# The first LayerNorm of an encoder layer: scale and offset with tokens as rows on half the columns, and the first loads in one queue

## The chip, the cores and the metric

The kernel runs on one core of a Trainium2 chip. The metric is the device time of one execution in microseconds (us). Times before and after come from repeated executions; a profile comes from one execution recorded by the hardware profiler.

## The reference

The input x holds 512 tokens of 1024 numbers. The reference computes:

```
x = layer_norm(x, ln_in_g, ln_in_b)                  # this case
h = x @ w_in                                         # q, k, v, latents, gates
a = differential attention, 4 heads                  # part A
b = latent attention, 8 heads, own low-rank q, kv    # part B
c = dilated window attention, 3 groups of 4 heads    # part C
y = sum over branches of sigmoid(g + b_gate) * (branch @ w_branch)
x = layer_norm(alpha * x + y @ w_out)
x = layer_norm(alpha * x + moe(x))                   # 16 experts, top 2, and a shared one

layer_norm(x, g, b) = (x - mean) * rsqrt(var + 1e-5) * g + b
```

Only the first line is computed differently. Its output is used twice: as input of the projections, and in the residual sum alpha * x.

## The kernel before

The tokens lie in 4 chunks of 128 (`NT`), the 1024 columns in 8 blocks of 128 (`KB`). For a projection TensorE needs the normed x with columns as partitions, in a high and a low part of float32r: `xh` and `xl`, 128 x 8 x 512 each. A product is three matmuls (`mm3`, lines 133 to 135): high by high, high by low weights, low by high weights. Weights come from DRAM and are split in the same way: ScalarE copies the high part, VectorE or GpSimd subtracts for the low part.

The start (`ln_in`, `start_step`) runs an order written out by hand, the string `START`. A step has a letter, a chunk c and, for some, a half g of the columns (g = 0 is columns 0 to 511, named `och`; g = 1 is `ocl`):

- X loads a chunk (two DMAs on SP's queue), s takes statistics, r and q work out mean and 1/sqrt (r ends with a square root on ScalarE, q goes on with it on VectorE).
- n (ScalarE) computes (x - mean) / std in place. t transposes four blocks on TensorE into a PSUM bank. u (ScalarE) or U (VectorE) applies scale and offset, which are one number for each partition by then, to one block of 128 x 128 at a time, from PSUM into SBUF. h copies into `xh`, l or L subtracts into `xl`.
- W loads a third of the weight `w_b1` (1008, 1008 and 672 columns), w and v or V split it. m multiplies a chunk with it: 8 blocks of 3 matmuls of 336 columns, 24 for a chunk. e copies the result out.
- K steps run helpers: constants, loads of small vectors, masks, tables of the rotary embedding. Z stores the chunk, without scale and offset, in DRAM (`xn_dram`) for the residual.

After `START` follow `steps`, which walks `PLAN` (parts A, B, C; `P0` is the first block of values, `v_block(0)`, two banks of 48 matmuls of 256 columns), and `FILL`, work that has no hurry: the gates (G and g, 24 matmuls of 512 columns each into the one bank `gm`), branch projections (O, B) and the residual steps (R). From `START` on, a scheduler places these instructions by its own estimates; each engine then runs its list strictly in order. R0 to R7 (`residual`) read a chunk and half of `xn_dram`, multiply by the scale and add the offset on GpSimd, and store it again.

SP, ScalarE and GpSimd each have a queue that issues DMAs in order.

## Time and profile before

| | us |
|---|---|
| times of 3 runs | 942.04, 946.68, 946.85 |
| median | 946.68 |
| the profiled execution's own time | 947.56 |
| its span | 945.8 |
| TensorE busy | 888.0 (94%) |
| VectorE, ScalarE, GpSimd busy | 639.0, 458.1, 230.5 |
| mean granted TensorE clock | 0.985 of full speed |

The span is what the profiler sees from the first to the last instruction. The time of the execution is 1.8 us longer. TensorE is idle for 57.8 us of the span, and the lists of views that follow tell where.

### The profile page before, as it was taken

The page shows a single profiled execution, that of the slowest core. Times are in us where ns is not written, and L with a number is a line of the kernel's source. Part 1 is how long each engine was busy: PE and PEld are TensorE (multiplying, and loading weights), DVE is VectorE, ACT ScalarE, POOL GpSimd, SP SyncE. Part 2 cuts the span into 40 slices and gives each one's busy share as a digit, 9 for nine tenths or more (in the row PEclk, how much of TensorE's full clock was granted, in tenths as well). Part 3 has the DMA queues.
Part 4 walks back from the last instruction along what each step waited for, and adds up shares of the span by engine and source line. Part 5 has one row for each costly group of instructions (what it writes and reads, how often), then busy time and mean ns, then how long its engine had stood idle before and what let it go on. Part 6 is the DMA issues. An engine that isn't in the chain of part 4 may idle for free.

```text
span 945.8 us, 13734 instructions
## 1 busy us (share of the span) xinstructions
PE 888.0 (94%) x4916; PEld 737.6 (78%) x4916; DVE 639.0 (68%) x1316; ACT 458.1 (48%) x797; POOL 230.5 (24%) x220
## 2 busy tenths in 40 slices
PE   4899999978998999999999999899999899999994
PEld 3889988767877988877989889788998666667762
DVE  6757885535678777955756586737775667676776
ACT  6645755445366544642433254333334555566632
POOL 2122140031020013003323336504033212111033
PEclk9999999989999999998999999999999999999998
DMA  7343443243348444444664558468556599999962
GB/s 263 117 137 109 146 125 106 90 125 106 119 150 246 127 154 134 150 129 115 170 190 128 147 183 262 161 217 308 191 198 247 190 336 359 361 403 388 389 205 90
DMA packets 61287, 183.74 MB, mean 194 GB/s; under 512 B 9088, under 2 KB 9520, under 8 KB 53920
## 3 DMA queue, kind: packets, MB, share of 16 engines
q1 hardware_dynamic: 50912, 147.84, 47.5%
q0 software_dynamic: 9584, 32.88, 9.3%
q10 hardware_dynamic: 720, 2.11, 0.6%
q8 instruction: 40, 0.66, 0.3%
q14 instruction: 31, 0.25, 0.1%
HBM read 139.18 MB, written 31.82 MB: 181 GB/s over the span
## 4 chain that ended last, share of the span: by engine, by line
PE 52%; DVE 7%; issue 7%; DMA 6%; ACT 2%; POOL 2%; SPq 0%; ACTq 0%; POOLq 0%; DVEq 0%
PE mm L1495 11%; PE sc L1521 7%; PE mm L133 5%; PE mm L134 5%; PE mm L135 5%; PE gm L133 2%; PE gm L134 2%; PE gm L135 2%; DMA w<-ys_dram,r 1%; PE tr L599 1%; PE tr L363 1%; PE sc L134 1%; PE sc L133 1%; PE sc L135 1%; DMA g_dram<-gt 1%
## 5 line engine op out<-in xcount | busy, mean ns | idle before, releaser
L171 DVE TENSOR_TENSOR w<-w,w 128x1024 fp32r<-128x1024 f32 (+5 forms) x97 | 155.6, 1621 | 51.0 <-ACT w L170 50.8
L170 ACT ACTIVATE w<-w 128x1024 fp32r<-128x1024 f32 (+5 forms) x99 | 122.2, 1263 | 58.1 <-PE mm L134 21.4
L134 PE MATMUL mm<-w,xh 128*128 128x256 f32 (+1 forms) x384 | 111.4, 290 | 0.2 <-DVE w L433 0.2
L133 PE MATMUL mm<-w,xh 128*128 128x256 f32 (+1 forms) x384 | 111.5, 291 | 0.0
L135 PE MATMUL mm<-w,xl 128*128 128x256 f32 (+1 forms) x384 | 111.2, 290 | 0.1
L1495 PE MATMUL mm<-w,xgh 128*128 128x512 f32 x320 | 100.9, 397 | 0.0
L134 PEld LDWEIGHTS mm<-w,xh 128*128 128x128 f32 x384 | 73.8, 192 | 1.4 <-DVE w L433 0.5
L133 PEld LDWEIGHTS mm<-w,xh 128*128 128x128 f32 x384 | 73.7, 192 | 1.1 <-ACT w L429 0.3
L135 PEld LDWEIGHTS mm<-w,xl 128*128 128x128 f32 x384 | 73.7, 192 | 0.9 <-DVE xl L472 0.5
L1521 PE MATMUL sc<-w,hT 128*128 128x512 f32 x160 | 73.2, 599 | 0.0
L1495 PEld LDWEIGHTS mm<-w,xgh 128*128 128x128 f32 x320 | 58.4, 188 | 11.0
L133 PE MATMUL mm<-xh,w 128*128 128x512 f32 x160 | 63.7, 398 | 0.9 <-DVE V L171 0.9
L134 PE MATMUL mm<-xl,w 128*128 128x512 f32 x160 | 63.6, 397 | 0.0
L135 PE MATMUL mm<-xh,w 128*128 128x512 f32 x160 | 63.3, 396 | 0.0
L1495 PE MATMUL mm<-w,xgl 128*128 128x512 f32 x160 | 62.5, 390 | 0.0
L170 ACT ACTIVATE pth<-tr 128x512 fp32r<-128x512 f32 x80 | 41.6, 548 | 35.4 <-PE tr L599 35.3
L588 ACT ACTIVATE e<-sc,nm 128x512 f32<-128x512 f32 x64 | 43.6, 685 | 29.9 <-DVE nm L659 17.0
L171 DVE TENSOR_TENSOR ptl<-tr,pth 128x512 fp32r<-128x512 f32 x80 | 48.8, 629 | 12.8 <-ACT pth L170 12.4
L170 ACT ACTIVATE T<-T 128x512 fp32r<-128x512 f32 (+1 forms) x36 | 22.7, 629 | 61.3 <-POOL T L571 39.0
L950 POOL DMA_DIRECT2D g_dram<-gt x24 | 13.7, 571 | 156.7 <-ACT gt L941 115.6
L1521 PEld LDWEIGHTS sc<-w,hT 128*128 128x128 f32 x160 | 29.0, 190 | 29.3 <-issue 27.7
L170 ACT ACTIVATE ghi<-graw 128x512 fp32r<-128x512 f32 x40 | 23.6, 625 | 52.3 <-PE gm L134 33.6
(445 smaller groups left out, 2284.6 us busy)
## 6 DMA issues: line engine op xcount, KB each, us to landing
w<-in_w_exp SPq DMA_DIRECT2D x48, 1024.0 KB, 7.7
graw<-in_w_gate SPq DMA_DIRECT2D x48, 256.0 KB, 3.0
T<-T SPq DMA_DIRECT2D x90, 128.0 KB, 2.5
w<-in_w_qk SPq DMA_DIRECT2D x20, 512.0 KB, 3.9
g_dram<-gt POOLq DMA_DIRECT2D x40, 256.0 KB, 3.2
w<-in_w_v SPq DMA_DIRECT2D x16, 512.0 KB, 4.0
ys_dram<-ys POOLq DMA_DIRECT2D x13, 512.0 KB, 7.8
gt<-g_dram SPq DMA_DIRECT2D x24, 256.0 KB, 2.8
```

The costliest lines, as they stand in the source:

```text
L133: nc.tensor.matmul(out, lh, rh, start=start, stop=False)
L134: nc.tensor.matmul(out, lh, rl, start=False, stop=False)
L135: nc.tensor.matmul(out, ll, rh, start=False, stop=stop)
L170: nc.scalar.activation(hi, src, AF.Copy)
L171: (eng or nc.vector).tensor_sub(lo, src, hi.bitcast(F32))
L363: nc.tensor.transpose(o.bitcast(FR), s.bitcast(FR), self.idr)
L588: nc.scalar.activation(out, src, AF.Exp, bias=nmax, scale=scale, accum_out=sm)
L599: nc.tensor.transpose(p[:, kb * 128:(kb + 1) * 128], e[:, kb * 128:(kb + 1) * 128], self.idf)
L950: self.nc.gpsimd.dma_start(self.g_dram[n // 8, n % 8, 0], self.gate(n, t == "g"))
L1495: self.nc.tensor.matmul(p, x[:, kb], y, start=kb == 0 and i == 0, stop=kb == KB - 1 and i == 2)
L1521: self.nc.tensor.matmul(y, hT[:, k], w[:, k, cs], start=k == 0, stop=k == 1)
```

## The change

For half g = 0 the scale and offset are applied while tokens are still rows. There they differ from column to column, so each must stand in all 128 partitions. A new step R loads the first 512 numbers of both vectors as one row (two KB each) by ScalarE's queue; b multiplies a column of ones by that row on TensorE, which leaves the row in all partitions of a PSUM bank (scale in `pv`, offset in `gm`). Then y computes (x - mean) * scale and z computes that * (1/std) + offset, both on VectorE with 128 x 512 elements. Steps n and u fall away for this half: the transposed block is final, so h and l read it from PSUM. Half g = 1 goes the old way, with u on ScalarE for all four chunks.

What Z stores for half 0 is then final, and R0 to R3 leave `FILL`. The loads of x and of `w_b1` are the first 12 DMAs of SP's queue; the small vectors and `lam` are issued by GpSimd. The chunks' matmuls (m) are cut at block 3 instead of 4, take the two `mm` banks in turn for all four chunks, and stand between the steps of the next chunk. The low parts of the weights come from GpSimd for all three thirds.

```
--- before.py
+++ after.py
@@ -47,7 +47,7 @@
 THETA = 500000.0
 DT = ()
 WIDE = (21,23)
-START = ("K0 G0 X0 s0 r0 q0 W0 w0 n01 X1 t01 X2 s1 W1 n00 r1 q1 u01 K1 n11 s2 t00 u00 n10 t10 X3 W2 V0 r2 q2 w1 V1 h00 s3 n20 l00 h01 u10 l01 r3 h10 t11 n21 t20 w2 v2 m00 U11 h11 L10 m01 q3 t21 m10 U20 U21 n31 n30 t31 L11 t30 h20 h21 l20 u31 U30 h30 h31 L21 m11 l30 m20 m21 l31 m30 m31 e0 e1 e2 e3 Z00 Z01 Z10 Z11 Z20 Z21 Z30 Z31")
+START = ("R0 X0 X1 G0 W0 K0 X2 W1 X3 W2 K6 K1 a0 b0 b1 s0 r0 y0 q0 z0 n01 s1 w0 t00 V0 h00 r1 t01 s2 u01 w1 q1 V1 y1 h01 l00 w2 z1 m00 n11 l01 V2 r2 t10 y2 t11 h10 q2 m01 u11 l10 z2 h11 m10 s3 n21 e0 t20 l11 t21 h20 r3 m11 y3 u21 l20 q3 z3 h21 m20 e1 n31 l21 t30 t31 h30 m21 u31 l30 h31 m30 e2 l31 m31 e3 K9 Z00 Z01 Z10 Z11 Z20 Z21 Z30 Z31")
 
 
 def ROPE(nc):
@@ -55,9 +55,9 @@
 
 
 RES = 4
-PLAN = ("k6 k2 P0 k3 k5 k7 L0 K0 K1 A0 K2 K3 L1 A1 P1 K4 K5 A2 k8 K6 K7 N T A3 J0 Q0 Y0 Q1 J1 Q2 H0 H1 Q3 Y1 k4 H2 H3 P2 H4 H5 K8 K9 H6 H7 P3 K12 K13 C0 K10 K11 P4 C1 K14 K15 P5 K18 K19 P6 C2 F K16 K17 P7 C3")
-
-FILL = ("G2 G0 g1 g3 G4 g5 G6 g7 G8 g13 g11 O0 G10 g9 O1 G12 O2 g15 O3 B2 B1 G14 B3 B0 g17 O4 G16 O5 O6 O7 B5 B7 B4 B6 / R0 R1 R2 R3 R4 R5 R6 R7 G18 g19 g21 g23 G22 G20")
+PLAN = ("P0 k2 k3 k5 k7 L0 K0 K1 A0 K2 K3 L1 A1 P1 K4 K5 A2 k8 K6 K7 N T A3 J0 Q0 Y0 Q1 J1 Q2 H0 H1 Q3 Y1 k4 H2 H3 P2 H4 H5 K8 K9 H6 H7 P3 K12 K13 C0 K10 K11 P4 C1 K14 K15 P5 K18 K19 P6 C2 F K16 K17 P7 C3")
+
+FILL = ("G2 G0 g1 g3 G4 g5 G6 g7 G8 g13 g11 O0 G10 g9 O1 G12 O2 g15 O3 B2 B1 G14 B3 B0 g17 O4 G16 O5 O6 O7 B5 B7 B4 B6 / R4 R5 R6 R7 G18 g19 g21 g23 G22 G20")
 LAST = ("r0 r1 Q00 Q01 Q02 Q03 c l3 l4 l5 m0 s0 u0 m1 s1 u1 w3 m2 x0 y0 l6 i0 s2 u2 b3 m3 x1 y1 l7 i1 s3 u3 b4 m4 x2 y2 s4 u4 b5 m5 x3 y3 s5 u5 b6 m6 x4 y4 s6 U6 b7 m7 x5 y5 i2 s7 U7 x6 y6 i3 x7 y7 A00 A01 A02 r2 e r3 g Q10 Q11 Q12 Q13 B00 B01 B02 P03 Q20 Q21 Q22 Q23 P10 P11 P12 P13 Q30 Q31 Q32 Q33")
 ORDER = ("u0 m u1 P20 P21 P30 a0 A0 P22 g0 P31 a1 A1 P23 g1 P32 T0 a2 A2 P33 b g2 a3 T1 A3 R0 M0 g3 R1 c T2 s0 N0 R2 f0 s1 T3 M1 R3 r N1 M2 f1 h0 N2 k o0 M3 i0 f2 h1 o1 N3 i1 S10 f3 D0 X h2 S11 h3")
 E0 = 4
@@ -209,12 +209,12 @@
 
     def cols(self, name, n, src=None):
         t = self.cp.tile([128, n], F32, name="v_" + name)
-        self.nc.sync.dma_start(t, self.a[name] if src is None else src)
+        self.nc.gpsimd.dma_start(t, self.a[name] if src is None else src)
         return t
 
     def loads(self):
         self.pos = self.cp.tile([128, NT], I32, name="pos")
-        self.nc.sync.dma_start(self.pos, self.a["positions"])
+        self.nc.gpsimd.dma_start(self.pos, self.a["positions"])
         self.inv = self.cols("inv_freq", 24, self.a["inv_freq"].to_broadcast([128, 24]))
 
     def loads2(self):
@@ -222,8 +222,11 @@
         self.dng = self.cols("diff_norm_g", 1)
         self.qng = self.cols("mla_q_norm_g", 3)
         self.kng = self.cols("mla_kv_norm_g", 2)
-        self.lam = self.T().bitcast(F32)[:, :256].rearrange("p (a b) -> p a b", a=4)
-        self.nc.sync.dma_start(self.lam, self.a["lam"].to_broadcast([128, 256]))
+
+    def scales(self):
+        nc = self.nc
+        nc.vector.tensor_scalar(self.hbg, self.hbg, 0.5, None, op0=OP.mult)
+        nc.vector.tensor_scalar(self.dng, self.dng, 1.0 - LAM_INIT, None, op0=OP.mult)
 
     def rope_tables(self):
 
@@ -334,9 +337,9 @@
         self.mk = mk
 
     def vectors(self):
-        nc, cp, lam = self.nc, self.cp, self.lam
-        nc.vector.tensor_scalar(self.hbg, self.hbg, 0.5, None, op0=OP.mult)
-        nc.vector.tensor_scalar(self.dng, self.dng, 1.0 - LAM_INIT, None, op0=OP.mult)
+        nc, cp = self.nc, self.cp
+        lam = self.T().bitcast(F32)[:, :256].rearrange("p (a b) -> p a b", a=4)
+        nc.gpsimd.dma_start(lam, self.a["lam"].to_broadcast([128, 256]))
         pr = self.T().bitcast(F32)[:, :128].rearrange("p (a b) -> p a b", a=2)
         nc.vector.tensor_mul(pr, lam[:, 0:4:2, :], lam[:, 1:4:2, :])
         sm = cp.tile([128, 2], F32, name="lam_s")
@@ -408,11 +411,36 @@
             return lp.tile([128, n], F32, name=f"{name}{c}")
 
         if t == "K":
-            (self.consts, self.loads, self.vectors, self.rope_tables, self.masks, self.rope_sin, self.loads2, self.rope_T, self.rope_L)[c]()
+            (self.consts, self.loads, self.vectors, self.rope_tables, self.masks, self.rope_sin, self.loads2, self.rope_T, self.rope_L, self.scales)[c]()
         elif t == "X":
             d["x", c] = [self.op.tile([128, S], FR, name=n, bufs=4).bitcast(F32) for n in ("och", "ocl")]
             for i in range(2):
-                nc.sync.dma_start(d["x", c][i], a["x"].rearrange("(i c) d -> c i d", c=NT)[c][:, i * 512:(i + 1) * 512])
+                nc.sync.dma_start(
+                    d["x", c][i], a["x"].rearrange("(i c) d -> c i d", c=NT)[c][:, i * 512:(i + 1) * 512])
+        elif t == "R":
+
+            d["gb"] = lp.tile([128, 2, 512], F32, name="gb")
+            nc.scalar.dma_start(d["gb"][0:1], a["ln_in"].rearrange("p (a b) -> p a b", a=2)[:, :, :512])
+            d["one"] = lp.tile([128, 128], F32, name="one")
+            v.memset(d["one"], 1.0)
+        elif t == "a":
+
+            nc.scalar.activation(small("sq"), d["one"][:, 0:1], AF.Sqrt)
+        elif t == "b":
+
+            d["b", c] = (self.pv_bank, self.gm_bank)[c]()
+            nc.tensor.matmul(d["b", c], d["one"][0:1], d["gb"][0:1, c], start=True, stop=True)
+        elif t == "y":
+            x = d["x", c][0]
+            v.scalar_tensor_tensor(x, x, d["mv", c][:, 0:1], d["b", 0], op0=OP.subtract, op1=OP.mult)
+        elif t == "z":
+            x = d["x", c][0]
+            v.scalar_tensor_tensor(x, x, d["rs", c], d["b", 1], op0=OP.mult, op1=OP.add)
+        elif t == "p":
+
+            d["warm"] = d.get("warm") or self.sc_bank()
+            for _ in range(c):
+                nc.tensor.matmul(d["warm"][:, :128], self.idf, self.idf, start=True, stop=True)
         elif t == "G":
             d["gc"] = lp.tile([128, 2, KB], F32, name="gc")
             nc.scalar.dma_start(d["gc"], a["ln_in_c"].rearrange("p (a b) -> p a b", a=2))
@@ -423,7 +451,8 @@
             else:
                 d["W", c] = [self.wstart(a["w_b1"][:, c * 1008:(c + 1) * 1008], 1008)[:, :1008]]
         elif t == "w":
-            d["w", c] = [self.slot_tile(i)[:, :1008 if c < 2 else 672] for i in (1, 2)]
+            d["w", c] = [(self.slot_tile(i + 1) if c < 2 else self.wp.tile([128, 1024], FR, name=n, bufs=1))[:, :1008 if c < 2 else 672]
+                         for i, n in enumerate(("ghi", "glo"))]
             for i, w in enumerate(d["W", c]):
                 n = w.shape[1]
                 nc.scalar.activation(d["w", c][0][:, i * n:(i + 1) * n], w, AF.Copy)
@@ -473,8 +502,8 @@
         elif t == "Z":
             nc.sync.dma_start(self.xn_dram[c][:, g * 512:(g + 1) * 512], d["x", c][g])
         elif t == "m":
-            p = d["m", c] = d.get(("m", c)) or (self.mm_bank, self.mm_bank, self.pv_bank, self.gm_bank)[c]()
-            for kb in range(4 * g, 4 * g + 4):
+            p = d["m", c] = d.get(("m", c)) or self.mm_bank()
+            for kb in range(3) if g == 0 else range(3, KB):
                 w = d["w", kb // 3]
                 self.mm3(p[:, :336], self.xh[:, kb, sl], self.xl[:, kb, sl], w[0][:, kb % 3], w[1][:, kb % 3], kb == 0, kb == KB - 1)
         elif t == "e":

```

Which instructions stand where is told by each engine's list.

SP's queue, from its first DMA, before (`och`, `ocl` are halves of a chunk, `w0` a third of `w_b1`):

```order
L415 DMA och_91<-in_x 128x512
L415 DMA ocl_92<-in_x 128x512
L212 DMA v_b_gate_433<-in_b_gate 128x24
L212 DMA v_diff_norm_g_435<-in_diff_norm_g 128x1
L212 DMA v_mla_q_norm_g_437<-in_mla_q_norm_g 128x3
L212 DMA v_mla_kv_norm_g_439<-in_mla_kv_norm_g 128x2
L153 DMA w0_111<-in_w_b1 128x1008
L415 DMA och_117<-in_x 128x512
L415 DMA ocl_118<-in_x 128x512
L415 DMA och_126<-in_x 128x512
L415 DMA ocl_127<-in_x 128x512
L153 DMA w0_134<-in_w_b1 128x1008
```

SP's queue after:

```order
L418 DMA och_87<-in_x 128x512
L418 DMA ocl_88<-in_x 128x512
L418 DMA och_91<-in_x 128x512
L418 DMA ocl_92<-in_x 128x512
L153 DMA w0_97<-in_w_b1 128x1008
L418 DMA och_105<-in_x 128x512
L418 DMA ocl_106<-in_x 128x512
L153 DMA w0_109<-in_w_b1 128x1008
L418 DMA och_111<-in_x 128x512
L418 DMA ocl_112<-in_x 128x512
```

The six small loads between the loads of x and `w_b1` are gone from this queue, and the second chunk stands ahead of the first weights.

VectorE, from the statistics of the third chunk, before (`st` statistics, `mv` mean and variance, `rs_y` 1/std, `nm` -mean/std):

```order
L438 BN_STATS st_159<-ocl 128x6
L234 CAST posf<-pos 128x4
L440 BN_AGGR mv_160<-st_159 128x2
L106 TENSOR_SCALAR rs_v<-mv_160 128x1
L113 RECIPROCAL rs_y<-rs_y 128x1
L116 TENSOR_SCALAR rs_t<-rs_y 128x1
L118 TENSOR_SCALAR rs_t<-rs_t,rs_v 128x1
L120 TENSOR_SCALAR rs_y<-rs_t,rs_y 128x1
L450 TENSOR_SCALAR nm_198<-mv_160,rs_y 128x1
L438 BN_STATS st_205<-och 128x6
L438 BN_STATS st_205<-ocl 128x6
L472 TENSOR_TENSOR xl<-u,xh 128x4x128 x2
```

VectorE after, from the statistics of the third chunk:

```order
L467 BN_STATS st_181<-och 128x6
L467 BN_STATS st_181<-ocl 128x6
L113 RECIPROCAL rs_y<-rs_y 128x1
L116 TENSOR_SCALAR rs_t<-rs_y 128x1
L237 CAST posf<-pos 128x4
L118 TENSOR_SCALAR rs_t<-rs_t,rs_v 128x1
L120 TENSOR_SCALAR rs_y<-rs_t,rs_y 128x1
L479 TENSOR_SCALAR nm_197<-mv_157,rs_y 128x1
L435 SCALAR_TENSOR_TENSOR och<-och,mv_157,pv 128x512
L501 TENSOR_TENSOR xl<-tr,xh 128x4x128
L438 SCALAR_TENSOR_TENSOR och<-och,rs_y,gm 128x512
L501 TENSOR_TENSOR xl<-u,xh 128x4x128
```

The first `xl` stood behind the statistics of all four chunks. Now it stands behind those of three, and behind the second chunk's first scaling step.

TensorE, its first rows, before (`tr`, `sc` banks for transposes, `mm` the product):

```order
L457 MATMUL tr<-idf,ocl 128x128 x4
L457 MATMUL tr<-idf,och 128x128 x4
L457 MATMUL sc<-idf,och 128x128 x4
L457 MATMUL sc<-idf,ocl 128x128 x4
L457 MATMUL tr<-idf,och 128x128 x4
L133 MATMUL mm<-w_113,xh 128x336
L134 MATMUL mm<-w_114,xh 128x336
L135 MATMUL mm<-w_113,xl 128x336
```

TensorE after (`gb` the row of scale and offset, `one` the ones):

```order
L432 MATMUL pv<-gb,one 128x512
L432 MATMUL gm<-gb,one 128x512
L486 MATMUL tr<-idf,och 128x128 x4
L486 MATMUL tr<-idf,ocl 128x128 x4
L133 MATMUL mm<-w_160,xh 128x336
L134 MATMUL mm<-w_161,xh 128x336
L135 MATMUL mm<-w_160,xl 128x336
```

Five groups of transposes, of three chunks, stood ahead of the first product. Now the two spreading matmuls and the two groups of the first chunk do. Further down, in the list after, twelve matmuls of `v_block(0)` stand inside the fourth chunk's product; before, that block's first matmul follows the fourth chunk's last.

## Rows read from the trace of the kernel before

**Rows 1.** The page: span, and busy time of TensorE.
```profile
span 945.8 us, 13734 instructions
...
PE 888.0 (94%) x4916; PEld 737.6 (78%) x4916; DVE 639.0 (68%) x1316; ACT 458.1 (48%) x797; POOL 230.5 (24%) x220
```

**Rows 2.** Windows: length, busy PE, PEld, DVE, ACT, POOL (count), clock, DMA share, GB/s.
```profile
0.00:20.00 20.00, 6.91 (x30) 5.68 (x31) 12.27 (x40) 12.93 (x27) 5.08 (x7) 1.00 0.83 279
20.00:40.00 20.00, 17.15 (x100) 16.12 (x99) 12.90 (x38) 13.08 (x28) 4.84 (x5) 0.91 0.34 115
40.00:60.00 20.00, 20.00 (x139) 18.58 (x138) 14.36 (x41) 10.33 (x19) 1.25 (x5) 1.00 0.40 131
```

**Rows 3.** Waits of TensorE, 0 to 130 us: total, times, longest.
```profile
PE tr L457 <- ACT ocl L453: 9.2, 1, 9.2
PE sc L457 <- ACT och L453: 3.5, 1, 3.5
```

**Rows 4.** Timeline of the start: start, length, engine, line, operation, idle and releaser.
```profile
1.66 0.42 SPq L212 DMA_DIRECT2D v_b_gate<-in_b_gate  x1
...
3.74 0.69 DVE L438 BATCH_NORM_STATS2 st<-och 128x6 f32<-128x512 f32 x1 [2.27 <-DMA och<-in_x]
...
5.79 0.16 DVE L113 RECIPROCAL rs_y<-rs_y 128x1 f32<-128x1 f32 x1 [0.27 <-ACT rs_y L111]
...
6.74 0.21 DVE L450 TENSOR_SCALAR nm<-mv,rs_y 128x1 f32<-128x1 f32 x1
...
7.42 1.04 ACT L429 ACTIVATE w<-w 128x1008 fp32r<-128x1008 f32 x1 [1.66 <-DMA w<-in_w_b]
...
9.22 1.11 PE L457 MATMUL tr<-idf,ocl 128*128 128x128 f32 x4 [9.22 <-ACT ocl L453]
...
17.06 2.19 DVE L472 TENSOR_TENSOR xl<-u,xh 128x512 fp32r<-128x512 f32 x2
...
18.70 0.45 PE L135 MATMUL mm<-w,xl 128*128 128x336 f32 x1
...
36.30 0.32 PE L133 MATMUL gm<-w,xh 128*128 128x336 f32 x1
...
40.01 0.40 PE L133 MATMUL mm<-w,xh 128*128 128x256 f32 x2
...
51.63 0.40 PE L133 MATMUL gm<-xh,ghi 128*128 128x512 f32 x1
```

**Rows 5.** TensorE after its pause: length, busy, clock, DMA share, GB/s; two timeline rows.
```profile
30.00:32.00 2.00, 2.00 (x9) 0.50 0.83 257
...
29.92 0.48 PE L135 MATMUL mm<-w,xl 128*128 128x336 f32 x1
...
30.20 0.48 PE L133 MATMUL mm<-w,xh 128*128 128x336 f32 x1
```

**Rows 6.** Groups by line: ScalarE and VectorE operations that the change drops or adds.
```profile
L464 ACT ACTIVATE u<-tr,gc x8: 448/462/483, 10.4 to 13.5; 128x128 f32<-128x128 f32 x8
...
L1193 DVE SCALAR_TENSOR_TENSOR x<-x,sc x8: 680/686/689, 738.6 to 817.6; 128x512 f32<-128x512 f32 x8
...
L470 ACT ACTIVATE xh<-u 128x512 fp32r<-128x512 f32 x8 | 4.8, 628 | 2.1 <-DVE u L466 2.0
...
L171 DVE TENSOR_TENSOR ptl<-tr,pth 128x512 fp32r<-128x512 f32 x64 | 43.2, 684 | 12.8 <-ACT pth L170 12.4
```

**Rows 7.** GpSimd's own DMA issues: a group, and times to landing of line 682.
```profile
L950 POOL DMA_DIRECT2D g_dram<-gt x24 | 13.7, 571 | 156.7 <-ACT gt L941 115.6
...
DMA to landing us min/median/max: 2.3/2.8/3.2
```

**Rows 8.** Windows of 20 us, three later stages, columns as in rows 2.
```profile
200.00:220.00 20.00, 15.14 (x62) 12.01 (x63) 8.57 (x15) 10.48 (x17) 6.77 (x7) 0.83 0.54 159
...
280.00:300.00 20.00, 15.51 (x79) 12.98 (x80) 17.24 (x43) 12.50 (x25) 3.88 (x6) 0.91 0.82 226
...
600.00:620.00 20.00, 17.56 (x95) 14.46 (x94) 14.00 (x28) 8.26 (x17) 4.04 (x5) 1.00 0.63 206
```


## The prediction

> **What bounds the kernel now.** I read the page first: TensorE is busy 888.0 of 945.8 us [rows 1], so time is lost only where TensorE stands still or runs slowly. The windows of 20 us show where. The first two hold 6.91 and 17.15 us of work, together 15.9 us idle; from 40 us on TensorE is full [rows 2], and the two windows after that row read the same. A start that ends earlier should therefore move everything behind it.
>
> The waits name who is late: TensorE waits 9.2 us for the first normed half and 3.5 us for the second chunk's, both from ScalarE's line 453 [rows 3]. In the timeline the first product lacks its `xl` until 18.70 and the start's last product ends at 40.01, where `v_block(0)` begins; its 96 matmuls run without a gap until 51.63, 0.121 us each [rows 4]. The last chunk's 24 matmuls take from 36.30 to 40.01, 0.155 us each [rows 4]. After the pause ahead of 28 us they came every 0.28 us, with a granted clock of 0.50, which is 1.2 GHz [rows 5].
>
> **The chain to the first `xl`.** I follow VectorE's list after the change, with durations of before. The first statistics begin at 3.74 and the reciprocal at 5.79, after an idle 0.27 for the square root [rows 4]. So statistics, aggregation and the first addition are 1.78 us of VectorE, and end at 5.52. Step y comes next, 0.69 us (a two-operation instruction with one operand in PSUM took 686 ns [rows 6]); the square root hides behind it. At 6.21 follow the five small steps of q, 5.79 to 6.95 before [rows 4], 1.16 us: 7.37. Step z, 0.69: 8.06. Chunk 1's statistics, 1.78: 9.84. Chunk 2's two, 2 x 0.69: 11.22. Chunk 1's q, with a cast more, 1.4: 12.6. Its y, 0.69: 13.3. Then the first `xl`, 0.68 (a subtraction with one operand in PSUM, 684 ns [rows 6]): 14.0. The others are beside this: the transposes, 1.11 us before [rows 4], end at 9.2, `xh` (628 ns [rows 6]) at 9.8. The weights' low part, after n, w and GpSimd, is at about 11.6.
>
> The loads allow this. The first weights arrived at 7.42 before [rows 4], behind four small loads, whose issues (0.42 us each [rows 4]) go; in their place stands the second chunk, 0.5 MB, 1.9 us at the first window's 279 GB/s [rows 2]. That is a draw, and they are wanted at 8.2. The spreading matmuls need two KB twice, issued first of all, by 5.5 us.
>
> So the first triple starts at 14.0 instead of 18.70.
>
> **From there to the end of the start.** TensorE has 94 of 96 products left, 94 x 0.155 = 14.6 us; six groups of transposes, at half of 1.11, 3.3 us; and the 12 matmuls of `v_block(0)` that the new order puts ahead of the last product's end, 1.5 us. At full speed that ends at 33.4. Pace: after its pause before, TensorE worked at 0.28 per product from 28 to about 32 us [rows 5]. Four us at that pace cost 4 x 0.45 = 1.8. Waits for operands I put at 1.0: VectorE's own list from the first `xl` to the last holds 8 subtractions, 3 y, 3 z, 3 q, three aggregations, the last statistics, three copies and one weight split, some 14.7 us without a wait, so it would end at 28.7 and delays single steps only. ScalarE holds four u fewer (four blocks of 462 ns each [rows 6]).
>
> A point to weigh is what a subtraction for `xl` costs while GpSimd splits weights, as it does from 9 to about 17 us after the change. The nearest row in the start is two of them beside GpSimd in 2.19 us, 1.1 each, both operands in SBUF [rows 4]; with one operand in PSUM it took 684 ns elsewhere [rows 6]. The new ones of half 0 have one in PSUM, so I take 0.68; at 1.1 the first `xl` would come at 14.4, and the gain be 4.9. The Trainium skill ("GPSIMD Engine Reference", section "Specifications") says that GpSimd shares its SBUF interfaces with VectorE, and collides with instructions that have two SBUF inputs. By it half 0 stays at 0.68 and only half 1 pays; the two rows agree.
>
> Sum: 33.4 + 1.8 + 1.0 = 36.2 for the start and 12 matmuls of what follows. Before, that point is 40.01 + 1.45 = 41.5. Gain 5.3 us, with bounds of 3 (2 us more of waits) and 7 (hardly any slow pace).
>
> **What hangs on it.** `v_block(0)` lasts about 10 us longer, and the weights for the next products have their slot sooner, so TensorE stays fed. One new wait lies there: `lam` now comes through GpSimd's queue, issued after the last use of the start's tiles (near 31 us), and VectorE's copies of the fourth chunk's result stand behind it. GpSimd spends 571 ns on an issue, landing takes 2.3 to 3.2 us [rows 7], so `lam` is there by 35; VectorE waits 1 to 2 us. Behind it waits the second bank of `v_block(0)`, which TensorE wants at about 41, some 2 us after that copy. I count nothing; with that cover gone, 1 to 2 us. The six earlier small loads are wanted no sooner than 11 us, and cost GpSimd 3.4 us before its first weight.
>
> **The residual steps.** R0 to R3 take four multiplications and as many additions from GpSimd, and eight transfers of half a chunk, around 576 to 604 us. TensorE was idle 2.4 us in 600 to 620 [rows 8], partly for gate weights behind those stores. Between 0 and 2.4 us I take 0.5.
>
> **Sum.** 947.56 - 5.3 - 0.5 = 941.8 against the profiled execution's own time. That one lies 0.9 above the median, 946.68; between 940.9 and 941.8 I take **941.0**.
>
> **Rivals.**
> 1. *Half of the gain is handed back.* The scheduler's list has changed far beyond the start. Counted in it, when the 64th score matmul of part A is due, 360 matmuls of gates and branches have gone instead of 312; from there to the 24th score product of part B only 12 are left to fill, before 60. In 280 to 300 TensorE is idle 4.5 us even with them [rows 8]. Against it: 200 to 220, idle 4.9 us [rows 8], is where the extra ones now lie. If a third of 48 x 0.23 = 11 us comes out as new waits, 3.7 us go back: 945. If it all does: 953, slower.
> 2. *The lead closes holes as well.* The same 48 matmuls fill the idle 4.9 us and the slow clock (0.83) of 200 to 220 [rows 8], and part B isn't hurt: 4 us more, 937.
> 3. *The clock stays low.* Products come in four bursts between transposes; if the gaps keep TensorE at 0.28 per product, each us at that pace costs 0.45. The gain of 5.3 plus the 1.8 counted is used up by 16 us at that pace, until about 30; through the whole start (to 47) it ends 8 us later than before: slower, 955. For it: one pause, the one ahead of 28 us, was enough before [rows 5]. Against it: I find no gap above 2 us after 12. The Trainium skill ("TensorE: Matmul & The Clock Gate", Part 1) has the throttled state as the default, released by activity, which is this rival's mechanism. The trace agrees, with 0.50 after the pause [rows 5].
> 4. *The start isn't shorter*, since the loads set it after all: x and weights are 3.5 MB, 12.5 us at 279 GB/s, and the fourth chunk is wanted at 21. Nothing speaks for it.
>
> **Chances.** The forecast (gain of 4 to 8) 0.57, rival 1 in its mild form 0.20, rival 2 0.12, rival 1 in full or rival 3 as slower 0.08, rival 4 0.03. A measurement here can tell 0.5%, 4.7 us, from no change. The forecast lies at that edge, a little beyond: two thirds of its chance count as faster, with rival 2 that is 0.50; slower 0.08; the same 0.42. The range goes from rival 2 to past rival 1's mild form, 936 to 948; the forecast's own is 938.5 to 943.5.
>
> **What would show it.** In the profile after: first statistics near 3.7, the first product's `xl` near 14, the start's last product near 36, no TensorE idle from there to 100, granted clock 1.00 from 20 us on. The lead in `v_block(0)` should then stand at the same 5 us at its end (near 46). A VectorE wait for a GpSimd load near 34 of 1 to 2 us, and nothing on TensorE from it. The prediction is wrong if the lead is there at 100 us and gone by 320 (rival 1), or if 14 to 36 shows a clock of 0.5 (rival 3).

## The result and the profile after

The changed kernel takes 954.1 us (median of 20 runs, 949.3 to 962.42), the kernel before 945.99 beside it: a ratio of 1.0088 (95% interval 1.0070 to 1.0105). It is 8 us slower; forecast were 941.0, faster. The profiled execution has a span of 951.5 us against 945.8 [rows 1]. The medians below leave out one execution each of e2, e10 and e11 that took far longer than the others of its kernel.

The page of the changed kernel, span and TensorE:

```profile
span 951.5 us, 13717 instructions
...
PE 895.5 (94%) x4920; PEld 741.4 (78%) x4920; DVE 633.8 (67%) x1310; ACT 457.1 (48%) x794; POOL 222.3 (23%) x218
```

Its windows of 20 us (columns as in [rows 2]):

```profile
0.00:20.00 20.00, 11.11 (x30) 7.34 (x31) 14.60 (x41) 10.36 (x20) 11.58 (x17) 1.00 0.84 265
20.00:40.00 20.00, 20.00 (x138) 19.97 (x138) 13.91 (x37) 15.89 (x36) 0.55 (x2) 1.00 0.45 156
...
80.00:100.00 20.00, 18.70 (x109) 16.90 (x108) 13.40 (x37) 11.75 (x30) 0.00 (x0) 1.00 0.43 117
160.00:180.00 20.00, 16.46 (x79) 12.95 (x77) 9.49 (x22) 11.78 (x21) 2.64 (x4) 1.00 0.25 76
200.00:220.00 20.00, 18.58 (x93) 14.94 (x92) 4.72 (x8) 10.23 (x15) 5.36 (x7) 1.00 0.30 104
280.00:300.00 20.00, 16.49 (x96) 14.05 (x96) 18.50 (x48) 13.35 (x26) 1.91 (x4) 0.91 0.86 266
400.00:420.00 20.00, 16.34 (x77) 12.51 (x76) 13.11 (x33) 10.25 (x25) 1.80 (x3) 0.94 0.29 89
420.00:440.00 20.00, 16.85 (x72) 13.56 (x72) 9.72 (x24) 6.51 (x13) 0.81 (x2) 0.80 0.12 34
440.00:460.00 20.00, 17.87 (x85) 15.07 (x84) 12.69 (x20) 4.86 (x6) 11.31 (x7) 0.97 0.58 160
600.00:620.00 20.00, 20.00 (x114) 17.28 (x113) 11.83 (x32) 10.08 (x20) 1.62 (x3) 1.00 0.54 171
```

Where these stages were full, or less empty, before:

```profile
80.00:100.00 20.00, 20.00 (x122) 18.71 (x121) 14.91 (x41) 12.58 (x35) 0.10 (x1) 1.00 0.29 86
160.00:180.00 20.00, 20.00 (x98) 16.23 (x98) 12.95 (x30) 11.94 (x21) 2.27 (x4) 1.00 0.28 95
400.00:420.00 20.00, 19.83 (x103) 16.21 (x102) 12.52 (x27) 10.25 (x21) 2.27 (x4) 1.00 0.49 152
420.00:440.00 20.00, 17.05 (x69) 13.13 (x68) 8.99 (x17) 4.55 (x10) 3.98 (x3) 0.83 0.20 61
440.00:460.00 20.00, 19.26 (x111) 16.86 (x110) 13.72 (x29) 7.54 (x11) 8.15 (x5) 1.00 0.65 177
```

The start gained: TensorE is idle 8.9 us in the first 40 us instead of 15.9 [rows 2], though partly at half pace. In 600 to 620 the idle 2.4 us of [rows 8] are gone. The loss lies between: 1.3 us in 80 to 100, 3.5 in 160 to 180, and in 400 to 460 it is idle 8.9 us instead of 3.9.

To follow the gain I count, for each profile, when TensorE has a given amount of work behind it (every matmul of the trace counted at its usual interval, the two new spreading products left out). The lead over the profile of the kernel before, in us, minus is behind; the first row is the time at which the kernel before has that much behind it:

```
time in the kernel before     82   165   217   309   392   483   564   670   921
changed                      4.3   2.1   7.8   5.1   3.5  -5.7  -6.6  -3.5  -5.5
e1 (changed, G18)            5.2   2.4   6.4   0.6  -1.0   1.5   0.6 -11.8 -12.4
e2 (before, G18)             2.2   2.4   2.4   3.7   3.7  10.7   8.2  -5.7  -8.1
e5 (changed, three behind)   4.8   3.2   7.1  -3.6  -3.0  -5.4  -5.4  -2.3  -2.5
e6 (before, three behind)    1.9   2.2   2.7   8.9   9.6   9.8   9.8   8.7   6.3
e9 (changed, sixth held)     5.6   3.4  -4.1  -2.9  -3.8  -5.2  -5.2  -2.1  -5.5
e15 (changed, both holds)    4.2   2.0   5.5  12.7  13.3  10.8  10.8  13.2  11.0
e16 (before, both holds)     3.3   0.7   4.1  12.9  13.5  13.5   9.9   8.6   6.1
e17 (e15 with R0 to R3)      4.4   2.1   5.4  14.7  15.3  14.3  13.2  12.4   7.1
```

The changed kernel is 4.3 us ahead at 82 and still 3.5 at 392; it loses 9 us between there and 483, gains 3 before 670, and loses 2 again. The start varies from profile to profile: over the ten with the changed start (without e13, where a further load delays it) the lead at 82 is 4.2 to 6.2, mean 5.0; over the eight with the old start (without e14) 0 to 3.3, mean 1.5. So the start is worth about 3.5 us on the average, not 5.3. Three of the eight old starts (before, e3, e18) show 3.4 us at a granted clock of 0.50 behind their pause, near 30 us, and have leads of 0 to 1.0; the other five show none ahead of 170 us and have 1.0 to 3.3. The profile on which the prediction was worked out is one of the three.

Filler behind it, as counted in the traces (products of 512 columns into `gm`; part A's score products have 128 x 512, part B's 96 x 512). Time / products gone:

```
                        before     changed    e9         e15        e16        e17
part A, 48th score   176.7/120  187.8/167  177.0/120  168.6/ 96  169.9/ 96  168.4/ 96
part A, 62nd         242.5/288  253.2/348  245.9/288  237.4/285  238.8/285  237.4/285
part B, 24th         299.4/348  303.1/372  302.5/348  292.2/336  291.2/336  289.4/336
part B, 72nd         377.3/444  385.8/480  381.1/444  367.2/456  366.9/456  365.1/456
part C, first        418.0/532  423.9/537  422.1/532  407.4/534  407.2/534  405.4/534
```

Part A's 48th score product comes 11.1 us later in the changed kernel with 47 products more gone (47 x 0.23 = 10.8 us). Towards part B's end it has nothing left: SyncE's queue stands from 409.54 at a load that needs part B's last heads, against 419.47 before. The queue's rows, changed kernel and then before:

```profile
409.54 25.68 SPq L993 DMA_DIRECT2D gt<-out_dram  x2
```

```profile
419.47 11.28 SPq L964 DMA_DIRECT2D gt<-out_dram  x2
```

And TensorE waits there for part B's own chain (waits of the changed kernel, 400 to 460):

```profile
PE sc L882 <- issue: 2.1, 1, 2.1
PE sc L133 <- ACT e L617: 1.7, 2, 1.5
PE pv L858 <- ACT pth L170: 1.6, 3, 0.7
```

### The profile page after: what moved, and what is told of

Read it like the earlier page. It is cut to its first block, busy times and chain, and to the rows that moved or that the text cites. A ratio compares the mean times of both kernels' runs of the same rounds, so it can differ in the third digit from the quotient of the medians.

```text
span 951.5 us, 13717 instructions
## 1 busy us (share of the span) xinstructions
PE 895.5 (94%) x4920; PEld 741.4 (78%) x4920; DVE 633.8 (67%) x1310; ACT 457.1 (48%) x794; POOL 222.3 (23%) x218
## 4 chain that ended last, share of the span: by engine, by line
PE 58%; DVE 6%; DMA 5%; issue 5%; ACT 2%; POOL 1%; SPq 0%; ACTq 0%; DVEq 0%; POOLq 0%
PE mm L1524 11%; PE sc L1550 7%; PE mm L135 6%; PE mm L133 6%; PE mm L134 6%; PE gm L133 3%; PE gm L135 3%; PE gm L134 3%; PE tr L628 2%; DMA w<-ys_dram,r 1%; PE tr L366 1%; PE pv L135 1%; PE pv L134 1%; PE pv L133 1%; PE sc L133 1%
## 5 line engine op out<-in xcount | busy, mean ns | idle before, releaser
L133 PE MATMUL mm<-w,xh 128*128 128x256 f32 (+1 forms) x392 | 115.6, 295 | 2.5 <-ACT xh L499 1.5
L134 PE MATMUL mm<-w,xh 128*128 128x256 f32 (+1 forms) x392 | 114.7, 293 | 1.3 <-POOL w L462 1.3
L135 PE MATMUL mm<-w,xl 128*128 128x256 f32 (+1 forms) x392 | 114.7, 293 | 1.2 <-DVE xl L501 1.2
L133 PEld LDWEIGHTS mm<-w,xh 128*128 128x128 f32 x392 | 76.5, 195 | 4.1 <-ACT xh L499 1.9
L134 PEld LDWEIGHTS mm<-w,xh 128*128 128x128 f32 x392 | 76.3, 195 | 2.3 <-POOL w L462 1.6
L135 PEld LDWEIGHTS mm<-w,xl 128*128 128x128 f32 x392 | 76.0, 194 | 2.0 <-DVE xl L501 1.6
L171 DVE TENSOR_TENSOR T<-T 128x512 fp32r<-128x512 f32 (+1 forms) x36 | 25.7, 715 | 26.5 <-ACT T L170 26.4
```

The costliest lines, as they stand in the source:

```text
L133: nc.tensor.matmul(out, lh, rh, start=start, stop=False)
L134: nc.tensor.matmul(out, lh, rl, start=False, stop=False)
L135: nc.tensor.matmul(out, ll, rh, start=False, stop=stop)
L171: (eng or nc.vector).tensor_sub(lo, src, hi.bitcast(F32))
```

## The experiments

All are compared with the kernel before on the same chip; ratios have their 95% interval. The edits are to the lists `FILL` or `START`, or a hold: a load of 4 bytes of a head's stored output into a gate's weight tile, ahead of the weight itself.

**First set: filler moved between the lists.** Theory 1 was that the start's lead is real and lost because filler runs out at part B's end.

e1 and, in the kernel before, e2:

```
-... O4 G16 O5 O6 ... / ... R7 G18 g19 ...
+... O4 G16 G18 O5 O6 ... / ... R7 g19 ...
```

> The changed kernel with one gate that depends on nothing late (G18, 24 products of 512 columns, 24 x 0.23 = 5.5 us) taken from the second list of filler and put ahead of O5 in the first. Theory 1 (the start's lead is real and is lost because the filler that needs nothing late is used up before part B ends): TensorE's idle time in 400 to 460, 8.9 us in the changed kernel, falls to about 4, as in the kernel before (3.9); the time falls by 4 to 6 us, to 948 to 950, and the lead over the kernel before is still there at 490 us. Rival (the lists are reshuffled everywhere and the loss is scatter, or comes from the start): within 2 us of 954, idle in 400 to 460 still 8 or more, or moved to another place.

> The kernel before with the same gate moved in the same way. Theory 1: part B's end has enough filler there already (idle 3.9 us in 400 to 460), so at most 1 to 3 us are gained of that idle time and some are given back later, where the gate is missing: 943 to 947, less than half of what the move gives the changed kernel. Rival (any move of filler shifts the time by as much): the gain is as large as in the changed kernel, 4 us or more.

e3 takes G16 out of the first list of the kernel before and puts it behind R7 in the second:

> The kernel before with G16, one gate that depends on nothing late, taken out of the first list of filler and put at the head of the gates of the second: the lack of 24 products that the changed kernel has at the end of part B, without the new start. Theory 1: new idle time of 4 to 6 us in 400 to 460 and a time of 949 to 952. Rival: the same as before within 2 us, 944 to 948, and no new idle time there.

e4, one part alone: `dma_start` of `pos` and of `cols` on `nc.gpsimd` in the kernel before.

> The kernel before with one part of the change alone: positions and the small vectors loaded from GpSimd's queue instead of SyncE's, the start's order as it was. All theories that put the loss into the filler: 944 to 948, the lists of the other engines don't change. Rival (the six issues on GpSimd, or their transfers beside x and the weights, hold the start up): 1 to 3 us slower, and the first product's xl later than 18.7.

Measured: e1 957.9 (1.0118, 1.0086 to 1.0150), e2 959.0 (1.0137, 1.0100 to 1.0175), e3 951.5 (1.0061, 1.0036 to 1.0085), e4 946.7 (1.0014, 0.9997 to 1.0031). Windows of e1:

```profile
400.00:420.00 20.00, 20.00 (x106) 17.05 (x105) 12.97 (x32) 11.68 (x25) 2.31 (x4) 1.00 0.38 116
420.00:440.00 20.00, 15.67 (x82) 11.70 (x81) 11.88 (x29) 7.85 (x19) 1.15 (x2) 1.00 0.29 87
440.00:460.00 20.00, 20.00 (x99) 16.95 (x98) 13.73 (x23) 6.54 (x8) 11.03 (x7) 1.00 0.56 160
580.00:600.00 20.00, 17.57 (x125) 16.35 (x124) 12.66 (x19) 8.01 (x15) 12.47 (x10) 1.00 0.45 140
600.00:620.00 20.00, 15.93 (x73) 13.14 (x72) 11.10 (x28) 8.07 (x17) 3.31 (x4) 0.85 0.60 198
...
640.00:660.00 20.00, 17.66 (x75) 14.04 (x75) 10.87 (x14) 6.83 (x11) 8.83 (x10) 0.83 0.42 130
```

The gate did close part B's hole as expected (idle 4.3 instead of 8.9, clock 1.00), and was then missing at part C's end, where 12 us were lost, part of them to the lower clock after the pauses. In e2 the same move cost the kernel before 14 us at that place, where 943 to 947 had been expected. So filler is a stock, and both places need it. e3 is slower by its 6 us, but not where theory 1 said; windows of e3:

```profile
400.00:420.00 20.00, 15.59 (x82) 11.65 (x80) 12.38 (x28) 10.36 (x22) 1.28 (x3) 1.00 0.28 90
420.00:440.00 20.00, 20.00 (x89) 16.59 (x90) 11.69 (x18) 4.88 (x6) 8.99 (x7) 1.00 0.53 148
580.00:600.00 20.00, 15.54 (x73) 12.40 (x72) 16.76 (x36) 10.24 (x20) 12.18 (x11) 0.93 0.69 227
```

TensorE is idle 4.4 us in 400 to 440 where the kernel before was idle 3.1, with no loss of lead, and 4.5 in 580 to 600, where the kernel before had no idle time. Moving the loads to GpSimd costs nothing that can be told (e4).

**Second set: gates held back within the first list.** e5, and in the kernel before e6:

```
-... G10 g9 O1 G12 O2 g15 O3 B2 ...
+... G10 O1 O2 O3 G9 G12 G15 B2 ...
```

> The changed kernel with three gates of the first list (9, 12, 15) put behind O3, the load of part A's last head, which arrives only when part A is over. Nothing moves to the second list. In the new order 312 filler products instead of 360 stand ahead of part A's 64th score product, as in the kernel before, and 84 instead of 57 come between part B's 72nd score product and... counted the other way, 456 instead of 480 have gone at the 72nd. Theory 1 (the extra 48 were used in part A without closing idle time there, and lack at part B's end): the idle 8.9 us in 400 to 460 fall to 5 or less, part A's last output leaves some 8 us earlier than 284, no new idle time above 2 us in part A: 946 to 950. If the whole start's lead comes through, 943. Rival (the hole at part B's end has another cause, such as SyncE's queue standing at O5, or comes back elsewhere): 952 to 956.

> The kernel before with the same three gates put behind O3. Its list changes little by it (312 products at part A's end as before; 480 instead of 468 gone at part B's 72nd score product). Theory 1: within 3 us of 946, rather slower by 1 to 3 since 12 products fewer are left at part B's end. Rival (holding the gates is good in itself, whatever the start): faster by 3 us or more, as much as in the changed kernel.

e7 is the same with `G10 g9 O1 O2 O3 G12 G15 B2`:

> The changed kernel with only two gates (12, 15) put behind O3: 336 products instead of 360 at part A's end, but 480 gone at part B's 72nd score product, as in the changed kernel. Theory 1: what counts is what is left at part B's end, so about half of what three gates give, or less: 949 to 954, idle in 400 to 460 still 6 to 9 us. Rival (what counts is when part A ends): as much as with three gates.

e8, `START` with `R0 X0 G0 W0 X1` instead of `R0 X0 X1 G0 W0`:

> The changed kernel with the first weights loaded ahead of the second chunk of x instead of behind it. In the changed kernel ScalarE waits 1.79 us for those weights (until 10.52) and the first xl follows at 15.17. If the order of the two loads is what made the first xl later than forecast: weights there by 9, first product with xl 14 to 15, the time 1 us less or the same as 954. Rival (VectorE's own list and the GpSimd split of 2.3 us set it): the first xl moves by less than 0.5 us, or later, since the second chunk's statistics wait in its place; the time the same.

Measured: e5 948.3 (1.0023, 1.0004 to 1.0042), e6 941.0 (0.9943, 0.9919 to 0.9966), e7 951.7 (1.0069, 1.0048 to 1.0091), e8 955.1 (1.0098, 1.0071 to 1.0124). e5 gives the 6 us that theory 1 wanted, but e6 gives the kernel before 5 as well: its rival, that holding is good in itself, was right, and theory 1 fell as the cause of the difference. In e5 the idle time in 400 to 460 fell to 6.6 only (5 or less had been expected), at 483 it is as far behind as the changed kernel (table above), and the hole moved to 220 to 260 (idle 5.4 and 3.7 us in its two windows). e7 is in line with theory 1, and can't tell it from that rival. (The 312 in these expectations was my miscount: the kernel before puts 24 products of its start into the same bank, so its filler at part A's end is 288.) In e8 the first weights were copied at 8.50 instead of 10.52 and the first `xl` came hardly earlier; rows of e8 on ScalarE and TensorE:

```profile
8.50 1.03 ACT L458 ACTIVATE w<-w 128x1008 fp32r<-128x1008 f32 x1
```

```profile
15.66 0.65 PE L135 MATMUL mm<-w,xl 128*128 128x336 f32 x1 [3.02 <-DVE xl L501]
```

15.66 against 15.91: VectorE's own list sets it, with its waits for x (0.50, 0.28 and 1.47 us in e8).

**Third set: the same amount of filler as before.** e9 holds the sixth gate until part A's second head is stored; e10 is that and e5's edit; e11 and, in the kernel before, e12 hold the fifth gate. `FILL` has `g3 G4 D1 g5` in e9 and `g3 D1 G4` in e11; the first branch below stands in `fill`, the second in `side_raw` ahead of the weight's load:

```
 elif t == "D":
     self.hold = n
...
 if getattr(self, "hold", None) is not None:
     self.nc.sync.dma_start(t[0][:1, :1], self.out_dram[self.hold][:1, :1])
     self.hold = None
```

> The changed kernel, with the sixth gate's weights held until part A's second head has been stored (a transfer of 4 bytes from that output into the weight's tile goes ahead of its load). From part A's 48th score product on, the same number of filler products has then gone in the list as in the kernel before: 120, 288 at the 64th, 528 at part B's 96th, against 167, 360 and 537 in the changed kernel (counted without the 24 products of the start that the kernel before puts in the same bank, which my earlier counts of 312 and so on held by mistake). Theory 2: the 47 products too many that stand ahead of part A's 48th score product (10.8 us) come where TensorE has no idle time, and push back a chain that then takes some 236 us to part C whatever filler lies in it. Then the 48th comes at 177 instead of 188, part C's first at 411 to 416 instead of 424, and the time is that of before less the start's lead and less the two or three us of the residual steps: 938 to 943. Rival 1 (the loss comes with the changed start itself, or from another part of it): 950 to 955 still. Rival 2 (half and half): 945 to 948.

> The same, and the three gates 9, 12 and 15 behind O3 as well: from part A's 48th score product on the same counts as the kernel before with those three gates moved, which took 941.0. Theory 2: that time less the start's lead and the residual steps' gain: 933 to 937, faster than both kernels. Rival 1: 946 to 949, as the changed kernel with the three gates moved.

> The changed kernel with the fifth gate held instead of the sixth: 96 products at part A's 48th score product, 264 at the 64th, then as in the kernel before. Theory 2: the 48th score product another 5.5 us earlier (171), and the 24 products come back in part A's end and part B's start, in idle time or not: 935 to 943. Rival (a hold leaves TensorE without work): 945 or more.

> The kernel before with the fifth gate held in the same way; its list changes only in that 96 instead of 120 products stand ahead of part A's 48th score product. Theory 2: a chain that starts up to 5.5 us earlier, with the same filler behind it: 941 to 946. Rival (a hold, or the small transfer, helps or hurts by itself): more than 5 us either way.

Measured: e9 951.2 (1.0056, 1.0037 to 1.0076), e10 945.1 (0.9990, 0.9965 to 1.0016), e11 945.7 (1.0001, 0.9984 to 1.0017), e12 948.3 (1.0041, 1.0022 to 1.0060). e9's counts are those of the kernel before, part A's 48th score product came at 177.0 as theory 2 said, and only 3 of the 8 us came back: rival 1. e10 is far from theory 2 as well and close to its rival 1. e11 and e12 missed theory 2's ranges from above, and with their edit the changed start is the faster one, by 2.6 us: the sign of the pair hangs on the order. Windows of e9:

```profile
160.00:180.00 20.00, 14.00 (x52) 9.69 (x51) 10.97 (x32) 12.55 (x25) 2.63 (x4) 0.81 0.19 67
420.00:440.00 20.00, 16.34 (x61) 12.02 (x60) 9.30 (x22) 6.17 (x14) 1.03 (x2) 0.74 0.28 86
```

So the amount of filler is a part, and where it stands among part A's own steps the rest: here the hold left 6 us empty, with a mean granted clock of 0.81 (part of the window at 1.2 and part at 2.4 GHz). One such price shows in all profiles: the gates share one bank, and each that follows the last at once waits for its tanh on ScalarE. Waits between 140 and 230 us, changed kernel and then before:

```profile
PE gm L133 <- ACT gt L970: 7.8, 8, 2.5
```

```profile
PE gm L133 <- ACT gt L941: 4.0, 4, 1.6
```

In the changed kernel two of these waits are all that TensorE waits for in 160 to 180, the 3.5 us lost there:

```profile
PE gm L133 <- ACT gt L970: 3.5, 2, 2.5
```

**Fourth set: the same order behind both starts.** e13 adds one load to `X0` of the changed kernel, e14 the same ahead of `X0` in the kernel before:

```
 if c == 0:
     z = lp.tile([128, 16], F32, name="zz")
     nc.sync.dma_start(z, a["x"][:128, :16*8].rearrange("p (a b) -> p a b", b=8)[:, :, 0])
```

> The changed kernel with one more load in SyncE's queue behind the first chunk of x: 128 x 16 single elements of 4 bytes, read at a stride of 32 bytes, used by nothing. It holds up what stands behind it in the queue (second chunk, first weights) by some us (by how much the trace tells; I don't know it), while the lists of TensorE, ScalarE, GpSimd and the order of the loads stay the same. Theory 3 (with the order given, a later start comes through to the end nearly whole): the time grows by 0.6 to 1 of what the start is later, so with 4 us some 957 to 958. Rival 1 (something downstream takes the lead whatever the order, a chain of transfers or of part A): the time stays within 1 us of 954.

> The kernel before with the same load ahead of the first chunk of x; the lists stay the same. Theory 3: slower by 0.6 to 1 of what its start is later. Rival 1: the same as before within 1 us.

e15, and in the kernel before e16 (the start of the list was `G2 G0 g1`):

```
-FILL = ("G2 G0 g1 ... G10 g9 O1 G12 O2 g15 O3 B2 ...
+FILL = ("D0 G2 G0 g1 ... G10 O1 O2 O3 G9 G12 G15 B2 ...
```

> The changed kernel with the first gate of all held until part A's first head has been stored, and the three gates 9, 12 and 15 behind O3: no filler ahead of part A's 32nd score product, 96 at the 48th, 285 at the 64th. With the same edit in the kernel before, TensorE's list behind the start is nearly the same in both (56 of 4593 rows differ, against 1093 between the changed kernel and the one before). Theory 3 (lead and order are two things, and the order is what cost 12 us): this pair differs by the start's lead and the residual steps' gain alone, the changed start 3 to 6 us faster than e16, and this one at 936 to 943. Rival 1 (the changed start loses its lead by itself): the same as e16 within 1.5 us, or slower.

> The kernel before with the same two edits (the first gate held until part A's first head has been stored, gates 9, 12 and 15 behind O3). Theory 3: 3 to 6 us slower than e15, at 940 to 948. Rival 1: the same as e15 or faster.

e17 is e15 with `/ R0 R1 R2 R3 R4 R5` in `FILL`; e18 is the kernel before with `/ R4 R5`:

> e15's kernel with R0 to R3 back in their place in the second list of filler (they scale the first half a second time, so the residual is scaled twice: work for its time only). Behind the start its lists are those of e16. If the start's lead comes through (theory 3): 2 to 4 us faster than e16, 936 to 938. If the gain of e15 over e16 is the residual steps' alone: the same as e16 within 1 us, 939 to 941. In both, TensorE should be idle 2 us or more in 560 to 620 again, and part B's beginning (12th to 24th score product) 2.4 us shorter than in e15.

> The kernel before with R0 to R3 left out: the first half of the residual then misses the norm's scale and offset. If the residual steps are worth 3 us or more by themselves: 941 to 943, TensorE's idle 2.4 us in 600 to 620 gone. If they are worth what was forecast (0.5) or give as much back at part B's beginning, where the order changes: 944 to 946.

Measured: e13 956.1 (1.0109, 1.0073 to 1.0144), e14 946.9 (1.0026, 1.0003 to 1.0049), e15 936.1 (0.9898, 0.9864 to 0.9931), e16 939.9 (0.9927, 0.9900 to 0.9954), e17 938.3 (0.9909, 0.9879 to 0.9940), e18 943.6 (0.9984, 0.9962 to 1.0007).

e13's load delayed the first `xl` by 1.1 us only, and the time grew by 2.0; in e14 it came 1.8 us later and the time grew by 1.3. Both go theory 3's way, but the delay was too small to settle it. The row of e13:

```profile
17.00 0.65 PE L135 MATMUL mm<-w,xl 128*128 128x336 f32 x1 [1.69 <-DVE xl L504]
```

The pair e15 and e16 does more. Page and windows of e15, then a window of e17:

```profile
span 935.1 us, 13718 instructions
...
160.00:180.00 20.00, 18.35 (x91) 15.29 (x92) 12.06 (x28) 8.56 (x18) 1.63 (x3) 1.00 0.38 128
...
400.00:420.00 20.00, 15.46 (x78) 11.18 (x77) 12.20 (x28) 9.86 (x21) 1.69 (x3) 1.00 0.25 71
420.00:440.00 20.00, 19.38 (x89) 15.94 (x87) 12.56 (x18) 6.50 (x8) 10.33 (x6) 1.00 0.51 143
...
600.00:620.00 20.00, 20.00 (x119) 17.55 (x118) 8.44 (x14) 8.25 (x16) 1.86 (x4) 1.00 0.70 250
```

```profile
580.00:600.00 20.00, 17.57 (x88) 14.11 (x87) 15.20 (x24) 7.16 (x15) 10.78 (x10) 1.00 0.50 172
```

The same two edits took 5.8 us from the kernel before (945.65 to 939.9) and 18 from the changed one (954.1 to 936.1). With nearly one order behind both, the changed kernel is 3.8 us faster by the medians (2.7 by the ratios, whose intervals overlap; of the runs, taken on one chip, five of e15's six are faster than all seven of e16's) where it was 8 slower. If start and residual steps are worth the same behind either order, the difference, some 12 us, is the order's. e15 beats both kernels. Of the 3.8, e17, on another chip, puts 2.2 to the residual steps (its idle 2.4 us are back, at 580) and 1.6 to the start, neither of them clear of noise; e17 lies between its two expected ranges. e18 gives the residual steps 1.9, between its two ranges, and its interval still holds no change. In the profiles e17 is 1.5 us ahead of e16 at part A's 48th score product and 1.8 at part C's first: over those 237 us, with nearly one order, a lead stays what it is. At 921 it is 1.0. e15 loses 2.4 us to e16 between part B's 12th and 24th score product, where the lists differ without R0 to R3's loads: 29.8 us against 27.4, and 27.0 in e17, which has them. At part C's first score product e15 is 0.2 us behind e16, and in the two profiles its advantage arises behind that point, where the residual steps are missing. So it is not shown that the start itself makes the whole kernel faster; shown is that with this order it does not cost the 8 us.

## Why the prediction was wrong, step by step

- **First `xl` product at 14.0: it came at 15.91.** The weights and the spreading were not late enough to matter; VectorE's list was. Rows of the changed kernel's start:

```profile
3.54 2.04 PE L432 MATMUL pv<-gb,one 1*128 1x512 f32 x2 [3.54 <-DMA gb<-in_ln_in]
5.38 1.91 PE L432 MATMUL gm<-gb,one 1*128 1x512 f32 x2
...
15.91 0.65 PE L135 MATMUL mm<-w,xl 128*128 128x336 f32 x1 [1.24 <-DVE xl L501]
...
37.09 0.32 PE L135 MATMUL mm<-ghi,xl 128*128 128x336 f32 x1
```

```profile
5.04 0.69 DVE L467 BATCH_NORM_STATS2 st<-ocl 128x6 f32<-128x512 f32 x1 [0.57 <-DMA ocl<-in_x]
...
11.19 0.69 DVE L467 BATCH_NORM_STATS2 st<-och 128x6 f32<-128x512 f32 x1 [1.02 <-DMA och<-in_x]
...
12.93 1.06 DVE L237 CAST posf<-pos 128x4 f32<-128x4 int32 x1
...
15.17 0.68 DVE L501 TENSOR_TENSOR xl<-tr,xh 128x512 fp32r<-128x512 f32 x1
...
16.43 1.00 DVE L501 TENSOR_TENSOR xl<-u,xh 128x512 fp32r<-128x512 f32 x1
...
23.73 0.68 DVE L501 TENSOR_TENSOR xl<-u,xh 128x512 fp32r<-128x512 f32 x1
```

```profile
11.65 2.31 POOL L462 TENSOR_TENSOR w<-w,w 128x1008 fp32r<-128x1008 f32 x1 [6.86 <-ACT w L458]
```

  VectorE waited 0.57 us for the first chunk's second half and 1.02 for the third chunk's first, and the cast that I put at 0.24 took 1.06. The "draw" on the loads was lost by VectorE's waits for x, not by the weights (e8). The cast waited for GpSimd: it ended at 13.99, and GpSimd's split of weights, in which it began, at 13.96. In nine of the eleven profiles with the changed start (e13 among them) it is the same: the cast begins during a split, ends 0.02 to 0.03 us behind it and takes 0.50 to 1.50 us; in e8 and e17 no split runs beside it, and it takes 0.16. So the collision with GpSimd that I weighed for the subtraction was paid by the cast. The subtraction with an operand in PSUM took 0.68, as forecast, with GpSimd at work beside it (its next split ran from 14.54 to 16.87); the one with both in SBUF took 1.00, and 0.68 at 23.73, when GpSimd had no split. The Trainium skill ("GPSIMD Engine Reference", "Specifications") has instructions with two SBUF inputs collide with GpSimd; the trace agrees.
- **Gain of 5.3: it is about 3.5** (4.3 in the shown pair). The first `xl` came 1.9 us late, and the slow pace lasted until 21.4, 5.5 us instead of 4. The 41.5 of before held 3.4 us at a clock of 0.50 that most old starts do not show. TensorE had no gap from 15.9 to 80; forecast was none until 100, and 80 to 100 has 1.3 us.
- **`lam`: no wait.** Its load was issued at 18.99, not near 31, and VectorE's sums at 36.35 waited for nothing.
- **The residual steps, 0.5: about 2** (e18 1.9, e15 against e17 2.2, neither clear of noise alone; idle 2.4 gone in 600 to 620 in the changed kernel and in e18). Mis-sized; the 2.4 of [rows 8] was the upper bound.
- **"What hangs on it": this step failed.** It took the work behind the start as a fixed chain that a lead moves forward as a whole. The scheduler places that work anew when the start changes: 1093 of TensorE's 4593 rows stand elsewhere, and the order that came out is, by the pairs, some 12 us worse than the old one. That is rival 1's mechanism, which I gave 0.20 in a mild form, with three errors. I counted 360 against 312 products, where 288 is right, so 72 too many had gone and not 48; I named 280 to 300, where the idle time is 3.5 us instead of 4.5, and it was 400 to 460; and I priced it at a third of the products' time, where 9 us were lost there, more than the lead. The full form, 953 and slower, shared a chance of 0.08 with rival 3; the 954.1 lies next to it by luck, since its 11 us rest on the wrong count. The sign I named for it, a lead gone by 320, did not show: 5.1 us were left at 309.
- **Rival 2** was true where it was looked for: 200 to 220 is busy 18.58 at a clock of 1.00, against 15.14 at 0.83 [rows 8]. But 160 to 180 lost as much, in waits for the gates' bank: the filler moved the hole.
- **Rival 3** did not come: the pace of 0.28 ended at 21.4, not at 30 or later. **Rival 4** was wrong, the start is shorter, though waits for x cost VectorE 1.6 us.

Shown is that the order behind the start decides (the same edits are worth 5.8 us in one kernel and 18 in the other, and with close orders the changed kernel is no longer the slower one). Filler used too early is a part of it: equal counts gave 3 us back (e9, and e10 against e5). Which of the other moved rows in part A cost the rest is not settled; e9's new hole shows that equal counts are not an equal order.

## What to carry to other kernels

Where a scheduler or a planner orders the work, compare the whole order before and after a change, and price the change in a pair in which the order behind it is the same; otherwise one measures the order. Work that fills gaps is a stock: count how much is gone at fixed points of the main chain, and hold it back by a dependency until the gaps begin. A lead counts only where nothing ready is placed into it.

## What the runs showed of the hardware

The start's slow pace is not visible in the windows, which print a granted clock of 1.00 for it. The trace of the changed kernel has no entry of the granted clock ahead of 21.72 us, where the first one, of 1.00, begins; the windows count a stretch without an entry as 1.00. Products came every 0.28 us until 21.42 and every 0.155 behind it, and after its pause the kernel before had the same 0.28 with 0.50 granted, 1.2 GHz [rows 5]. In all twenty traces the products change from the slow to the fast pace where the first entry begins, between 18.49 and 24.45 us. So the start most likely ran at the lower of the two levels; that is read from the pace, not from an entry. Rows of the changed kernel:

```profile
21.14 0.48 PE L135 MATMUL mm<-w,xl 128*128 128x336 f32 x1
21.42 0.46 PE L133 MATMUL mm<-w,xh 128*128 128x336 f32 x1
21.70 0.33 PE L134 MATMUL mm<-w,xh 128*128 128x336 f32 x1
21.87 0.32 PE L135 MATMUL mm<-w,xl 128*128 128x336 f32 x1
```

A spreading product of one row and 512 columns, in float32, took 2.04 and 1.91 us in the start (rows in the section before), two records each, where a whole product of 128 rows and 336 columns took 0.28 at that pace. Waits that come from an order repeat: the wait of 2.50 us for the gates' bank near 173 is in the changed kernel, e1, e8 and e13 alike.
